# Two more hidden tiles ahead in each feed-forward input, a new load order for its output stage, and adaLN one block later

## The chip, the cores and the metric

One core of a Trainium2 chip runs the whole program. The metric is the device time of one execution in microseconds (us). TensorE (PE, its weight load PEld) multiplies matrices, VectorE (DVE), ScalarE (ACT) and GpSimd (POOL) work on elements, and SyncE (SP) issues all transfers of this program.

## What is computed

A trunk of two layers over 1024 frames of width 1024, everything in float32. Each layer has a mixer sublayer and a feed-forward sublayer, and each sublayer normalizes, shifts and scales by columns that come from the conditioning vector c (adaLN), and adds its gated result to x:

```python
cond = jax.nn.silu(c)
for layer in range(DEPTH):
    mod = cond @ ada_w[layer] + ada_b[layer]
    sh1, sc1, g1, sh2, sc2, g2 = jnp.split(mod, 6, axis=-1)
    h = modulate(rms_norm(x, ln_mix_g[layer]), sh1, sc1)
    ...
    x = x + g1[:, None, :] * mix
    h = modulate(rms_norm(x, ln_ffn_g[layer]), sh2, sc2)
    x = x + g2[:, None, :] * swiglu(h, ffn_w_in[layer], ffn_w_out[layer])

def swiglu(h, w_in, w_out):
    gate, up = jnp.split(h @ w_in, 2, axis=-1)
    return (jax.nn.silu(gate) * up) @ w_out
```

The hidden width is 2816, that is 22 tiles of 128. The mixers (attention and a state-space model in layer 0, retention and stick-breaking attention in layer 1) aren't touched by the change.

## The kernel before

**Layout.** x is kept transposed: eight tiles of 128 channels by 1024 frames. Each float32 operand of a product is split into a high and a low part of the type fp32r, and a product is three matmuls (`mm3`, lines 305 to 309): high by high, high by low, low by high. The split of an operand is a cast on ScalarE for the high part and a subtraction on POOL or VectorE for the low part.

**Weights.** `Stream` (lines 103 to 200) loads weights in the order of `plan` (line 266) into four `raw` buffers that it shares with the adaLN loads, and splits them into six `whl` buffers (lines 169 and 170). Each tick of `Pipe` (line 52) pumps it: it splits what has landed as far as `whl` buffers are free, and asks for loads as long as fewer than two wait.

**Feed-forward input.** For each hidden tile m of 128, `ffn_in` (line 1434) computes gate and up of both halves of the frames as a two by two block product in the manner of Strassen and Winograd: seven products in place of eight. Each is one call of `prod` (line 1406): four pairs of channels, three matmuls each, so 12 matmuls of 128x512. The weight sides are A11, A12, A22 and the sums S1 to S4 that `Comb.raw` (line 210) makes on VectorE (line 218); `Comb.make` splits them (lines 227 and 228) in groups of one or two, one `whl` buffer a group. The frame sides are the split normalized first half (HT, columns 0 to 511), and for the second half the sums T1 (kept in HT, channels 0 to 3), T2, T3, T4 and the second half itself (HT, channels 4 to 7). `norm_t` (line 416) makes these for the four pairs of channels, one after the other, with VectorE for the sums and `put` (line 428) for the splits, whose subtractions alternate between POOL and VectorE. All combine through PSUM banks: three of tag `mm`, four of tag `at`. The results go to memory as `ad` (line 1450).

**The early tiles.** A11 and A12 need only the first half of the frames. While the second half is being normalized, `ffn_first` (line 1410) does these two products for the first EARLY = 3 tiles, first all three of A11, then all three of A12, from weights loaded a second time as whole units (`wfirst`). Their sums stay in SBUF as `p1` and `sg`, three buffers each. `ffn_in` then does five products for these tiles (S2, S3, S1, A22, S4) and seven for the others.

**Feed-forward output.** `ffn_out` (line 1499) takes the hidden tiles in blocks of two, and four in the last block. For each block, half of the frames and output tile n it accumulates 6 matmuls in a bank and adds the bank to x (line 1537). The hidden tiles come back from `ad` into the eight HT buffers (line 1509), the last four into other buffers (line 1518), and x from `xd` into buffers that held T2 to T4 (line 1527). All these are issued on SP.

**adaLN.** `ada` (line 336) makes one of the six columns of a layer: eight loads of 512 KB, each multiplied into an accumulator on VectorE (lines 345 and 347), one a tick, then two ticks on a product with ones on TensorE (line 353). During layer 0's output stage `run` (line 1607) makes five columns of layer 1, one after the other; it is started ahead of the stage.

**What sets the order.** The program text gives the order in which the steps are written, with generators that advance by ticks. The tile framework then plans the order on each engine and queue with a clock of its own, within the data's and buffers' dependencies. Each engine and SP's queue run strictly in the planned order.

Of the kernel before, what the change touches and what calls it, by code (L numbers as in the profile page):

```python
# [17 lines left out]
P = 128  # L18
D = 1024
T = 1024  # L20
# [4 lines left out]
FB = 2  # L25
EARLY = 3
EPS = 1e-6
# [210 lines left out]
class Trunk:  # L238
    def __init__(self, ctx, tc, I, out):
# [17 lines left out]
        for name, shape in (("mixd", [NK, P, T]), ("cad", [P, 16, 2, P]), ("m2d", [P, 16, 2, P]), ("ed", [P, 16, 2, P]),  # L257
                            ("m1d", [P, 32, P]), ("kd", [16, 32, 16, 16]), ("ytd", [4, P, T]), ("vd", [8, P, NT, 64]),
                            ("qkd", [4, 2, 2, P, T]), ("xd", [NK, P, T]), ("ad", [NH, P, 2, T]), ("ud", [8, P, 512])):
            setattr(self, name, self.dr.tile(shape, F32, name=name))  # L260
# [5 lines left out]
    def plan(self):  # L266
# [11 lines left out]
        def ffn(l):  # L278
            w = I["ffn_w_in"][l]
            self.wfirst.append([st.unit(w[m].rearrange("p (k u c) -> p k u c", k=NK, u=2)[:, :, 0]) for m in range(EARLY)])  # L280
            some, full = (("S2", "S3"), ("S1", "A22"), ("S4",)), (("A11", "A12"), ("S2", "S3"), ("S1", "A22"), ("S4",))
            self.win.append([st.pairs(w[m], some if m < EARLY else full, m > 0) for m in range(NH)])
            self.wfo.append([st.unit(I["ffn_w_out"][l, m * P:(m + 1) * P, :]) for m in range(NH)])
# [52 lines left out]
    def ada(self, pool, layer, part):  # L336
# [3 lines left out]
        for k in range(NK + 1):  # L340
# [8 lines left out]
            yield 1  # L349
        yield 2  # L350
        ps = self.at_bank()
# [64 lines left out]
    def norm_t(self, pool, fp, ar, x, sb):  # L416
# [16 lines left out]
        for p in range(4):  # L433
# [9 lines left out]
            v.tensor_sub(t1, h12, b11.hi.bitcast(F32))  # L443
            v.tensor_sub(t1, t1, b11.lo.bitcast(F32))
            v.tensor_sub(t2, h22, t1)
            put(self.T[2][p], t2)
            v.tensor_sub(h12, h22, h12)
            put(self.T[3][p], h12)
            put(self.HT[:, p, sl], t1)
            v.tensor_sub(t4, b21.hi.bitcast(F32), t2)  # L450
# [959 lines left out]
    def ffn_first(self, layer, fp):  # L1410

        nc, pipe = self.nc, self.pipe
        first = slice(0, 512)
        w = [c.k(0) for c in self.wfirst[layer]]
        self.p1, self.sg = {}, {}
        for m in range(EARLY):
            ps = self.mm_bank()
            self.prod(ps, w[m], [self.HT[:, p, first] for p in range(4)])
            self.p1[m] = fp.tile([P, 512], F32, tag="p1", bufs=EARLY, name="p1")
            nc.scalar.copy(self.p1[m], ps)  # L1420
            pipe.tick()
        for m in range(EARLY):
            ps = self.mm_bank()
            self.prod(ps, w[m][:, 512:], [self.HT[:, 4 + p, first] for p in range(4)])
            self.gate(fp, m, self.p1[m], ps)
            self.wfirst[layer][m].free()
            pipe.tick()

    def gate(self, fp, m, p1, p2):
        self.sg[m] = fp.tile([P, 512], F32, tag="sg", bufs=EARLY, name="sg")  # L1430
        self.nc.vector.tensor_add(self.sg[m], p1, p2)
        self.nc.scalar.activation(self.sg[m], self.sg[m], AF.Silu)

    def ffn_in(self, layer, fp, tp):
# [8 lines left out]
        def tmp():  # L1443
            return fp.tile([P, 512], F32, tag="u", bufs=4, name="u")
# [7 lines left out]
        for m in range(NH):  # L1452
            w = self.win[layer][m]
            early = m < EARLY
            if not early:
                a = self.mm_bank()
                self.prod(a, w.get("A11"), b11)
                self.p1[m] = fp.tile([P, 512], F32, tag="p1", bufs=EARLY, name="p1")
                nc.scalar.copy(self.p1[m], a)
                pipe.tick()  # L1460
                a = self.mm_bank()
                self.prod(a, w.get("A12"), b21)
                self.gate(fp, m, self.p1[m], a)
                w.free("A12")
                pipe.tick()
            b = self.mm_bank()
            self.prod(b, w.get("S2"), self.T[2])
            u = tmp()
            v.tensor_add(u, self.p1[m], b)
            pipe.tick()  # L1470
            c = self.at_bank()
            self.prod(c, w.get("S3"), self.T[3])
            c22 = tmp()
            v.tensor_add(c22, u, c)
            w.free("S3")
            pipe.tick()
            d = self.at_bank()
            self.prod(d, w.get("S1"), t1)
            c21, c22 = c22, tmp()
            v.tensor_add(c22, c21, d)  # L1480
# [17 lines left out]

    def ffn_out(self, pool, ar, layer, x, done):

# [19 lines left out]

        for m in range(NK):
            load(m)
        for n in range(NK):
            k = n // 2 + n % 2 * 4
            x[k] = ar.tile([P, T], F32, tag="ar", bufs=12, name="x")
        for n in range(NK):
            nc.sync.dma_start(out=x[n], in_=self.xd[n])
        for bi, ms in enumerate(blocks):
            last = bi + 1 == len(blocks)
            for h in range(2):  # L1530
                sl = slice(h * 512, h * 512 + 512)
# [21 lines left out]
def build(ctx, tc, I, out):  # L1553
# [37 lines left out]
    def half_layer(layer, ar, x, late, before, done, adas=()):  # L1591
# [13 lines left out]
        with tc.tile_pool(name=f"ph2{layer}", bufs=1, reuse_waits="tile") as p2:  # L1605
# [4 lines left out]

            pipe.start(run())
            k.ffn_out(p2, ar, layer, x, lambda n, h: done(p2, n, h))
            if layer == 0:
# [142 lines left out]
```

## Time and profile before

| | us |
|---|---|
| median of 3 runs | 2605.24 |
| lowest, highest | 2605.15, 2607.04 |
| the profiled execution | 2606.74 |
| its span, first to last instruction | 2605.0 |

| engine | busy us | share of the span |
|---|---|---|
| TensorE | 2449.5 | 94% |
| VectorE | 1562.7 | 60% |
| POOL | 1091.8 | 42% |
| ScalarE | 890.8 | 34% |

The profile is of one execution. A row of the timeline gives the start and the length of an instruction and, in brackets, how long the engine stood idle before it and what released it. Matmuls overlap, so their lengths exceed the distance between their starts, and the distance is what counts. The granted clock is a share of 2.4 GHz; the other level, 1.2 GHz, reads 0.50, and a stretch with both lies between.

### The profile page before, as it was taken

The page shows a single profiled execution, that of the slowest core. Times are in us where ns is not written, and L with a number is a line of the kernel's source. Part 1 is how long each engine was busy: PE and PEld are TensorE (multiplying, and loading weights), DVE is VectorE, ACT ScalarE, POOL GpSimd, SP SyncE. Part 2 cuts the span into 40 slices and gives each one's busy share as a digit, 9 for nine tenths or more (in the row PEclk, how much of TensorE's full clock was granted, in tenths as well). Part 3 has the DMA queues.
Part 4 walks back from the last instruction along what each step waited for, and adds up shares of the span by engine and source line. Part 5 has one row for each costly group of instructions (what it writes and reads, how often), then busy time and mean ns, then how long its engine had stood idle before and what let it go on. Part 6 is the DMA issues. An engine that isn't in the chain of part 4 may idle for free. (4 is left out here: it accounts for less than half of the span.)

```text
span 2605.0 us, 33520 instructions
## 1 busy us (share of the span) xinstructions
PE 2449.5 (94%) x12384; PEld 2029.7 (78%) x12384; DVE 1562.7 (60%) x2474; ACT 890.8 (34%) x1679; POOL 1091.8 (42%) x772
## 2 busy tenths in 40 slices
PE   6999898997999998799999999999979999998999
PEld 4898676875888887578788788877758888887887
DVE  6576564368766663576541466666587666654553
ACT  4332467524333332000232344444244333331000
POOL 3465102436776765121123134243148676662220
PEclk9999999998999999899999999999989999999999
DMA  7287764541333336864145332234523333339311
GB/s 284 90 243 222 198 183 155 197 162 57 122 117 110 114 113 259 323 236 152 63 124 173 97 102 83 61 104 135 171 73 114 105 113 113 107 131 364 145 45 65
DMA packets 189812, 379.40 MB, mean 146 GB/s; under 512 B 37264, under 2 KB 91216, under 8 KB 184272
## 3 DMA queue, kind: packets, MB, share of 16 engines
q1 hardware_dynamic: 189648, 377.26, 43.0%
q8 instruction: 98, 1.61, 0.3%
q14 instruction: 66, 0.54, 0.1%
HBM read 278.89 MB, written 100.40 MB: 146 GB/s over the span
## 5 line engine op out<-in xcount | busy, mean ns | idle before, releaser
L170 POOL TENSOR_TENSOR whl<-raw,whl 128x1024 fp32r<-128x1024 f32 x98 | 242.1, 2489 | 602.4 <-ACT whl L169 505.7
L1537 DVE SCALAR_TENSOR_TENSOR x<-at,col,x 128x512 f32<-128x512 f32 x320 | 236.5, 749 | 196.9 <-PE at L309 196.8
L228 POOL TENSOR_TENSOR whl<-sw,whl 128x512 fp32r<-128x512 f32 x176 | 266.7, 1526 | 67.6 <-ACT whl L227 67.6
L307 PE MATMUL at<-a,whl 128*128 128x512 f32 x704 | 279.4, 397 | 16.4 <-DMA a<-ad 13.8
L308 PE MATMUL at<-a,whl 128*128 128x512 f32 x704 | 277.4, 394 | 0.0
L309 PE MATMUL at<-a,whl 128*128 128x512 f32 x704 | 277.0, 393 | 0.0
L308 PE MATMUL mm<-HT,whl 128*128 128x512 f32 x688 | 270.1, 393 | 0.2
L307 PE MATMUL mm<-HT,whl 128*128 128x512 f32 x688 | 268.8, 393 | 1.2 <-ACT p L1420 1.1
L309 PE MATMUL mm<-HT,whl 128*128 128x512 f32 x688 | 269.2, 392 | 0.0
L169 ACT CAST whl<-raw 128x1024 fp32r<-128x1024 f32 x116 | 119.3, 1052 | 437.1 <-PE at L309 200.6
L307 PE MATMUL mm<-whl,HT 128*128 128x512 f32 (+1 forms) x688 | 249.9, 364 | 9.7 <-ACT HT L504 9.2
L308 PE MATMUL mm<-whl,HT 128*128 128x512 f32 (+1 forms) x688 | 246.0, 358 | 0.0
L309 PE MATMUL mm<-whl,HT 128*128 128x512 f32 (+1 forms) x688 | 243.5, 358 | 0.0
L228 POOL TENSOR_TENSOR whl<-raw,whl 128x512 fp32r<-128x512 f32 x120 | 178.2, 1497 | 138.8 <-ACT whl L227 138.8
L218 DVE TENSOR_TENSOR sw<-raw 128x512 f32<-128x512 f32 x88 | 144.1, 1638 | 63.0 <-POOL whl L228 61.4
L307 PEld LDWEIGHTS at<-a,whl 128*128 128x128 f32 x704 | 134.3, 191 | 47.7 <-issue 14.9
L227 ACT CAST whl<-sw 128x512 fp32r<-128x512 f32 x176 | 104.9, 620 | 165.5 <-PE at L309 111.7
L307 PEld LDWEIGHTS mm<-whl,HT 128*128 128x128 f32 x688 | 138.3, 201 | 26.9 <-ACT HT L504 11.9
L309 PEld LDWEIGHTS at<-a,whl 128*128 128x128 f32 x704 | 134.2, 191 | 28.4
L308 PEld LDWEIGHTS at<-a,whl 128*128 128x128 f32 x704 | 134.3, 191 | 27.9 <-issue 0.2
L308 PE MATMUL at<-HT,whl 128*128 128x512 f32 x384 | 151.9, 396 | 0.9 <-DVE HT L430 0.9
L307 PEld LDWEIGHTS mm<-HT,whl 128*128 128x128 f32 x688 | 130.1, 189 | 29.0 <-ACT p L1420 1.6
(343 smaller groups left out, 5380.5 us busy)
## 6 DMA issues: line engine op xcount, KB each, us to landing
raw<-in_ffn_w_in SPq DMA_DIRECT2D x94, 512.0 KB, 3.6
ad<-aT SPq DMA_DIRECT2D x88, 512.0 KB, 3.0
raw<-in_ada_w SPq DMA_DIRECT2D x80, 512.0 KB, 4.6
a<-ad SPq DMA_DIRECT2D x36, 1024.0 KB, 10.7
raw<-in_ffn_w_out SPq DMA_DIRECT2D x44, 512.0 KB, 4.1
xd<-x SPq DMA_DIRECT2D x24, 512.0 KB, 2.7
x<-xd SPq DMA_DIRECT2D x24, 512.0 KB, 8.2
ada<-in_ada SPq DMA_DIRECT2D x16, 512.0 KB, 10.7
```

The lines of the kernel that those rows point to most:

```text
L169: nc.scalar.copy(hi, u.raw[:, :u.n])
L170: self.low.tensor_sub(lo, u.raw[:, :u.n], hi.bitcast(F32))
L218: self.stream.t.nc.vector.tensor_tensor(t, a, b, op)
L227: nc.scalar.copy(hi, z)
L228: nc.gpsimd.tensor_sub(lo, z, hi.bitcast(F32))
L307: mm(out, lhs.hi, rhs.hi, start=start, stop=False)
L308: mm(out, lhs.hi, rhs.lo, start=False, stop=False)
L309: mm(out, lhs.lo, rhs.hi, start=False, stop=stop)
L1537: nc.vector.scalar_tensor_tensor(xh, ps, self.col[layer, 5][:, n:n + 1], xh, M, A)
```

## The change

EARLY is 5 in place of 3. `ffn_first` weaves the products: A11 of tile m, then A12 of tile m - 1. `p1` and `sg` keep three buffers each; the results of all five tiles are stored to a tensor `pd` in memory, and `back` loads them again one tile ahead of their use. S1 is computed first of a tile's later products, T1 is split first in `norm_t`, and the groups become (S1, S2), (S3, A22), (S4). `ffn_out` loads a[0] and a[1], the first halves of x, a[2] and a[3], the second halves of x, then a[4] to a[7]. The chain of five adaLN columns starts with the second block of the output stage, and every adaLN column's product on TensorE comes a tick later.

```diff
-EARLY = 3
+EARLY = 5
...
+("pd", [EARLY, 2, P, 512]),
...
-            some, full = (("S2", "S3"), ("S1", "A22"), ("S4",)), (("A11", "A12"), ("S2", "S3"), ("S1", "A22"), ("S4",))
+            some, full = (("S1", "S2"), ("S3", "A22"), ("S4",)), (("A11", "A12"), ("S1", "S2"), ("S3", "A22"), ("S4",))
...
-        yield 2
+        yield 3
...
             v.tensor_sub(t1, t1, b11.lo.bitcast(F32))
+            put(self.HT[:, p, sl], t1)
             v.tensor_sub(t2, h22, t1)
             put(self.T[2][p], t2)
             v.tensor_sub(h12, h22, h12)
             put(self.T[3][p], h12)
-            put(self.HT[:, p, sl], t1)
...
-        for m in range(EARLY):
-            ps = self.mm_bank()
-            self.prod(ps, w[m], [self.HT[:, p, first] for p in range(4)])
-            self.p1[m] = fp.tile([P, 512], F32, tag="p1", bufs=EARLY, name="p1")
-            nc.scalar.copy(self.p1[m], ps)
-            pipe.tick()
-        for m in range(EARLY):
-            ps = self.mm_bank()
-            self.prod(ps, w[m][:, 512:], [self.HT[:, 4 + p, first] for p in range(4)])
-            self.gate(fp, m, self.p1[m], ps)
-            self.wfirst[layer][m].free()
-            pipe.tick()
+        for m in range(EARLY + 1):
+            if m < EARLY:
+                ps = self.mm_bank()
+                self.prod(ps, w[m], [self.HT[:, p, first] for p in range(4)])
+                self.p1[m] = fp.tile([P, 512], F32, tag="p1", bufs=3, name="p1")
+                nc.scalar.copy(self.p1[m], ps)
+                nc.sync.dma_start(out=self.pd[m, 0], in_=self.p1[m])
+                pipe.tick()
+            if m:
+                ps = self.mm_bank()
+                self.prod(ps, w[m - 1][:, 512:], [self.HT[:, 4 + p, first] for p in range(4)])
+                self.gate(fp, m - 1, self.p1[m - 1], ps)
+                nc.sync.dma_start(out=self.pd[m - 1, 1], in_=self.sg[m - 1])
+                self.wfirst[layer][m - 1].free()
+                pipe.tick()
+        self.back(fp, 0)
+
+    def back(self, fp, m):
+
+        if m < EARLY:
+            self.p1[m], self.sg[m] = (fp.tile([P, 512], F32, tag=t, bufs=3, name=t) for t in ("p1", "sg"))
+            for j, t in enumerate((self.p1[m], self.sg[m])):
+                self.nc.sync.dma_start(out=t, in_=self.pd[m, j])
...
         for m in range(NH):
             w = self.win[layer][m]
             early = m < EARLY
+            self.back(fp, m + 1)
...
+            d = self.at_bank()
+            self.prod(d, w.get("S1"), t1)
+            pipe.tick()
             b = self.mm_bank()
             self.prod(b, w.get("S2"), self.T[2])
             u = tmp()
             v.tensor_add(u, self.p1[m], b)
+            w.free("S2")
             pipe.tick()
             c = self.at_bank()
             self.prod(c, w.get("S3"), self.T[3])
-            c22 = tmp()
-            v.tensor_add(c22, u, c)
-            w.free("S3")
-            pipe.tick()
-            d = self.at_bank()
-            self.prod(d, w.get("S1"), t1)
-            c21, c22 = c22, tmp()
+            c21, c22 = tmp(), tmp()
+            v.tensor_add(c21, u, c)
             v.tensor_add(c22, c21, d)
             v.tensor_add(u, u, d)
             pipe.tick()
...
-        for m in range(NK):
-            load(m)
         for n in range(NK):
             k = n // 2 + n % 2 * 4
             x[k] = ar.tile([P, T], F32, tag="ar", bufs=12, name="x")
-        for n in range(NK):
-            nc.sync.dma_start(out=x[n], in_=self.xd[n])
+        for h in range(2):
+            for m in range(2 * h, 2 * h + 2):
+                load(m)
+            for n in range(NK):
+                nc.sync.dma_start(out=x[n][:, h * 512:h * 512 + 512], in_=self.xd[n, :, h * 512:h * 512 + 512])
+        for m in range(4, NK):
+            load(m)
         for bi, ms in enumerate(blocks):
             last = bi + 1 == len(blocks)
+            if bi == 1:
+                pipe.start(extra)
...
-            pipe.start(run())
-            k.ffn_out(p2, ar, layer, x, lambda n, h: done(p2, n, h))
+            k.ffn_out(p2, ar, layer, x, lambda n, h: done(p2, n, h), run())
```

## Rows read from the trace of the kernel before

**Rows 1.** The page's busy shares: busy us, share of the span, instructions.
```profile
PE 2449.5 (94%) x12384; PEld 2029.7 (78%) x12384; DVE 1562.7 (60%) x2474; ACT 890.8 (34%) x1679; POOL 1091.8 (42%) x772
```

**Rows 2.** What TensorE waited for: us in total, times, longest us.
```profile
PE mm L307 <- ACT T L429: 23.3, 4, 10.0
PE at L353 <- DVE ada L347: 17.9, 1, 17.9
...
PE at L307 <- DMA a<-ad: 13.8, 2, 7.1
```

**Rows 3.** Windows, each: PE, PEld, DVE, ACT, POOL busy us, clock, DMA share, GB/s.
```profile
622.00:632.00 10.00, 10.00 (x34) 8.02 (x33) 7.90 (x13) 5.39 (x9) 3.98 (x3) 0.72 0.00 0
...
658.00:677.00 19.00, 19.00 (x86) 15.73 (x85) 14.66 (x16) 6.74 (x12) 15.69 (x12) 1.00 0.39 139
```

**Rows 4.** Timeline of TensorE, layer 0, from the early products to the T stage.
```profile
592.86 0.39 PE L308 MATMUL mm<-HT,whl 128*128 128x512 f32 x1
593.09 0.40 PE L309 MATMUL mm<-HT,whl 128*128 128x512 f32 x1
...
604.38 1.22 PE L307 MATMUL mm<-T,whl 128*128 128x512 f32 x2 [10.03 <-ACT T L429]
```

**Rows 5.** Timeline of TensorE: output stages of layer 0 and 1, line 353 between.
```profile
1026.84 0.77 PE L307 MATMUL at<-a,whl 128*128 128x512 f32 x1 [6.74 <-DMA a<-ad]
...
1030.59 0.39 PE L307 MATMUL at<-a,whl 128*128 128x512 f32 x1
...
1076.55 3.57 PE L353 MATMUL at<-ones,ada 128*128 128x1 f32 x16 [17.90 <-DVE ada L347]
...
1085.12 0.40 PE L307 MATMUL at<-a,whl 128*128 128x512 f32 x1
...
2358.74 0.77 PE L307 MATMUL at<-a,whl 128*128 128x512 f32 x1 [7.09 <-DMA a<-ad]
...
2365.12 0.40 PE L307 MATMUL at<-a,whl 128*128 128x512 f32 x1
```

**Rows 6.** Timeline of TensorE, the same place in layer 1.
```profile
1936.21 1.22 PE L307 MATMUL mm<-T,whl 128*128 128x512 f32 x2 [9.46 <-ACT T L429]
```

**Rows 7.** Timeline of VectorE, layer 0, the T stage.
```profile
596.35 2.05 DVE L436 SCALAR_TENSOR_TENSOR nf<-x,col,at 128x512 f32<-128x512 f32 x3
...
600.24 1.76 DVE L447 TENSOR_TENSOR nf<-nf 128x512 f32<-128x512 f32 x1
...
607.96 0.68 DVE L447 TENSOR_TENSOR nf<-nf 128x512 f32<-128x512 f32 x1
...
629.22 0.68 DVE L451 TENSOR_TENSOR tn<-tn,HT 128x512 f32<-128x512 f32 x1
```

**Rows 8.** Windows, columns as in rows 3; under them one DMA issue of 1010:1070.
```profile
1010.00:1070.00 60.00, 41.92 (x177) 33.95 (x175) 27.31 (x35) 6.93 (x8) 14.97 (x8) 0.87 1.02 405
1080.00:1220.00 140.00, 137.40 (x621) 112.76 (x622) 104.57 (x131) 12.01 (x12) 27.60 (x12) 0.98 0.63 218
...
raw<-in_ada_w SPq DMA_DIRECT2D x8, 512.0 KB, 9.5
```

**Rows 9.** Timeline of SP's queue, layer 0, at the output stage's start.
```profile
1008.09 3.54 SPq L1527 DMA_DIRECT2D x<-xd  x5
...
1014.83 4.67 SPq L1509 DMA_DIRECT2D a<-ad  x4
```

**Rows 10.** Timeline of POOL, layer 0, early products and T stage.
```profile
572.32 3.69 POOL L170 TENSOR_TENSOR whl<-raw,whl 128x1024 fp32r<-128x1024 f32 x1 [16.57 <-ACT whl L169]
...
595.24 1.71 POOL L228 TENSOR_TENSOR whl<-sw,whl 128x512 fp32r<-128x512 f32 x1
...
612.36 1.28 POOL L430 TENSOR_TENSOR T<-nf,T 128x512 fp32r<-128x512 f32 x1 [6.68 <-DVE tn L450]
```

**Rows 11.** The page's DMA issues: count, KB each, median us to landing.
```profile
raw<-in_ffn_w_in SPq DMA_DIRECT2D x94, 512.0 KB, 3.6
ad<-aT SPq DMA_DIRECT2D x88, 512.0 KB, 3.0
```

More of the change, by code (lines that the diff above doesn't have):

```diff
@@ L258, in __init__ @@
                             ("m1d", [P, 32, P]), ("kd", [16, 32, 16, 16]), ("ytd", [4, P, T]), ("vd", [8, P, NT, 64]),
-                            ("qkd", [4, 2, 2, P, T]), ("xd", [NK, P, T]), ("ad", [NH, P, 2, T]), ("ud", [8, P, 512])):
+                            ("qkd", [4, 2, 2, P, T]), ("xd", [NK, P, T]), ("ad", [NH, P, 2, T]), ("pd", [EARLY, 2, P, 512]), ("ud", [8, P, 512])):
             setattr(self, name, self.dr.tile(shape, F32, name=name))
@@ L1415, in ffn_first @@
         self.p1, self.sg = {}, {}
-        for m in range(EARLY):
-            ps = self.mm_bank()
-            self.prod(ps, w[m], [self.HT[:, p, first] for p in range(4)])
-            self.p1[m] = fp.tile([P, 512], F32, tag="p1", bufs=EARLY, name="p1")
-            nc.scalar.copy(self.p1[m], ps)
-            pipe.tick()
-        for m in range(EARLY):
-            ps = self.mm_bank()
-            self.prod(ps, w[m][:, 512:], [self.HT[:, 4 + p, first] for p in range(4)])
-            self.gate(fp, m, self.p1[m], ps)
-            self.wfirst[layer][m].free()
-            pipe.tick()
+        for m in range(EARLY + 1):
[19 more added lines that the diff above has]
+                self.nc.sync.dma_start(out=t, in_=self.pd[m, j])
     def gate(self, fp, m, p1, p2):
-        self.sg[m] = fp.tile([P, 512], F32, tag="sg", bufs=EARLY, name="sg")
+        self.sg[m] = fp.tile([P, 512], F32, tag="sg", bufs=3, name="sg")
         self.nc.vector.tensor_add(self.sg[m], p1, p2)
@@ L1457, in ffn_in @@
                 self.prod(a, w.get("A11"), b11)
-                self.p1[m] = fp.tile([P, 512], F32, tag="p1", bufs=EARLY, name="p1")
+                self.p1[m] = fp.tile([P, 512], F32, tag="p1", bufs=3, name="p1")
                 nc.scalar.copy(self.p1[m], a)
@@ L1497, in ffn_in, with ffn_out @@
             pipe.tick()
-    def ffn_out(self, pool, ar, layer, x, done):
+    def ffn_out(self, pool, ar, layer, x, done, extra):
         nc, pipe = self.nc, self.pipe
```

## The prediction

> **What bounds the kernel now.** First the page's busy shares: TensorE runs 2449.5 of 2605.0 us [rows 1], so the end is set by TensorE and by its holes, and the reader should look for holes. Then the waits of TensorE, longest first [rows 2]: three causes lead. Products that read a T tile wait 23.3 us in four places; the small adaLN product of line 353 waits 17.9 us once; the first product of the output stage waits 13.8 us in two places. They are what the diff touches, and they are priced one by one from the timeline.
>
> The first: at the upper of TensorE's two clock levels, 2.4 GHz (granted 1.00 from 658 to 677 [rows 3]), matmuls start 0.23 us apart [rows 4], so a product of `prod` (12 matmuls) takes 2.8 us; behind a long hole they run for a while at 1.2 GHz, 0.43 us apart [rows 5]. After the six early products TensorE stands 10.03 us in layer 0 [rows 4] and 9.46 us in layer 1 [rows 6]; the rest of the 23.3, 3.8 us, are small holes further on. Behind this stands VectorE: it makes the T tiles from 596.35 to 629.9 with hardly a pause [rows 7]. The second and third lie in one stretch. From 1010 to 1070 the transfers fill the DMA engines (share 1.02, 405 GB/s, in 60 us 24.3 MB) [rows 8]: eight x loads are issued from 1008.09 on, the a tiles only from 1014.83 on [rows 9], and TensorE starts 6.74 us late; layer 1 repeats it with 7.09 us [rows 5]. In that jam lie also the eight adaLN loads of the first of five parts [rows 8], and line 353, placed in TensorE's order by the planner, holds everything behind it for 17.90 us [rows 5].
>
> **The change, part by part. 1: two more tiles early, in both layers.** Nothing is added to TensorE: tiles 3 and 4 do their first two products earlier. The four products are 4 x 12 x 0.23 = 11.0 us of work for a hole of 10.03 and of 9.46 us. If the T tiles come when they came, TensorE is through 11.0 us sooner: the little more than the hole is swallowed by the small holes behind it. S1 ahead of S2 asks for T1, which the norm now splits first; that can only make the first start earlier, and I give it nothing.
>
> What is paid: five early weights hold five of the six `whl` buffers, so of tile 0 only one group fits beside them, and tile 1's groups, which were finished beside the early products (the last subtraction starts at 595.24), get buffers only as the early weights fall free, that is within the T stage. Two more splits of 128x1024 go over POOL, 3.69 us for one here [rows 10]. In the T stage VectorE gets two gate additions and perhaps tile 1's four sums, all of the T operations' shape, and is slowed by five POOL subtractions: such an operation takes 0.68 us, or 1.76 [rows 7]. From below 0 (all of it falls behind the T work), from above 6 x 0.68 = 4.1 and some 2.7 us for half of the five subtractions meeting an operation: 6.8 us. I take 3, nearest to the two additions and two sums without POOL beside them. The other way, the low clock after the hole (0.72 from 622 to 632 [rows 3]) costs 2.8 us there at most. So each layer gains 11 - 3 = 8 us, bounds 4 and 14: **16 us, 8 to 28**.
>
> On why 0.68 becomes 1.76: the Trainium skill, page "SBUF — State Buffer", section "Who interferes with whom", says that a VectorE instruction with two inputs in SBUF and a GpSimd one that reads SBUF shut each other out for a whole instruction. The two lengths of line 447 agree. The rule speaks against this change, as POOL's work moves into the stage that VectorE paces; what it would do at its worst is rival 1.
>
> The spill: ten stores and ten loads of 256 KB a layer. A store of 512 KB lands 3.0 us after issue, a weight load after 3.6 [rows 11]; the loads are asked a tile ahead (five products, 13.8 us), and the DMA engines are mostly idle there (share 0.39 from 658 to 677 [rows 3]). Cost 0, from below 0, from above rival 3. Two more weight loads a layer, the same. In later early tiles TensorE wants a new tile every 13.8 us; POOL has for it five subtractions and two more for the result, 7 x 1.71 = 12.0 [rows 10]: it fits, with little to spare. In 658 to 677 POOL is busy 15.69 of 19 us [rows 3].
>
> **2: the output stage's order.** S1 first means that HT0 to HT3, which a[0] to a[3] go into, are free after the third product of the last tile and not after the fifth: 2 x 2.76 = 5.5 us sooner. Ahead of a[0], a[1] stood 4 MB of x, about 10 us at 405 GB/s; now nothing, and only x halves (2 MB) stand between the first a tiles and the next. a[0] and a[1] land before TensorE ends, the first x halves by the time of the first evacuation; the second halves are wanted 11 us on. Removed: 6.74 us, and the low clock behind it (9 matmuls in 3.75 us for 2.07: 1.7); in layer 1 7.09 us, and 15 matmuls in 6.38 for 3.45: 2.9 [rows 5]. Together 18.4. I keep 2 us for a start that isn't clean: **16 us, 10 to 18.4**; 10 is what the 5.5 us alone would bring in each layer, less clock.
>
> **3: adaLN a block later.** A block of the output stage is 96 matmuls, 22 us; `yield 3` moves line 353 one tick (12 matmuls) further. Line 353 is then wanted some 22 + 12 x 2.8 = 55 us after the stage's start, at about 1075 on the old scale. What must have moved by then is the 24.3 MB of the jam and some 3 MB more, 67 us at 405 GB/s from 1007 on: 1074. So it just fits, and the wait comes out at 0 to 5 us, not 18. The four later parts, with the DMA share at 0.63 [rows 8], have no wait at line 353 at all (one wait in the list [rows 2]). Gone with it: line 353's 16 small matmuls at the low clock (3.57 us, half of that at the high one: 1.8) and 12 matmuls from their end to 1085.12, 5.0 us for 2.8: 2.2 [rows 5]. 17.9 + 1.8 + 2.2 = 21.9, less 3 for a remaining wait: **19 us, 5 to 22**. The chain of five parts now takes 8 + 60 ticks of the stage's 88, so it still ends inside; the other five adaLN calls each end a tick later, at nothing, since none of them is waited for in [rows 2].
>
> **Sum.** 16 + 16 + 19 = 51 us, bounds 23 and 68. The profiled execution took 2606.7 us (its span of 2605.0 and 1.7 around it), so 2555.7; the median of the runs is 1.5 below that execution, so **2554 us**, bounds 2537 and 2582.
>
> **Rivals.** Rival 1, the T stage gives back what the early products bring: tile 1's subtractions and sums land among the T operations and push the last T tile back by the full 11 us. For it: VectorE has no pause there, and the 1.76 us beside POOL. Against: POOL is idle for 6.68 us at a time in that stage [rows 10], and the planner may put the sums behind. Part 1 brings nothing: 35 us, 2570.
>
> Rival 2, the adaLN wait moves on instead of going: the loads still come late, since line 353 is placed by a plan that didn't see the jam. For: the bytes just fit. Against: four later parts at a lower share without a wait. Part 3 brings 2 us: 34, 2571.
>
> Rival 3, on the slower side: the spill blocks SP's queue. A load from `pd` can only go once its store has landed, and everything behind it on SP, the next tile's weight rows above all, waits too. If each of ten early tiles waited for its own store and load, 3.0 + 3.6 = 6.6 us and half as much for the low clock, that is 99 us: 2653. It decides from 5.1 us a tile on, where it eats the 51. Against: the loads are asked 13.8 us ahead. The Trainium skill, page "DMA: Bandwidth & Descriptors", section "Two DMAs through the same engine are not ordered", says that the issuing engine has to wait for the first transfer's semaphore before it issues one that reads its bytes. No row of this trace shows how long SP stands for it.
>
> Rival 4, the change doesn't do what it says: the engines' order comes from the planner, not from the text; TensorE's rows in the T stage mix products of several tiles. If it sets x ahead of a again and the early products behind the T work, only part 3 is left: 19 us, 2587; at worst nothing.
>
> **How the numbers follow.** The forecast has 0.60, rival 1 0.13, rival 2 0.12, rival 3 0.07, rival 4 0.08. The range, 2536 to 2582, takes in the bounds of the sum and rivals 1 and 2. About 0.2%, 5 us, is what a measurement can tell from no change. Faster: 0.60 + 0.13 + 0.12 and 0.05 of rival 4 = 0.90; same: 0.03 of rival 4 and 0.01 of rival 3; slower: 0.06 of rival 3.
>
> **What would show it.** Part 1: ten products back to back before the first that reads T, no hole over 3 us there, the last T operation within 3 us of its old place. Part 2: a[0] and a[1] issued ahead of x, no wait for a at the stage's start. Part 3: line 353 under 5 us. Rival 1 shows as holes in TensorE between the first and the last T tile that grew by about 10 us, rival 3 as waits for `whl` or p1 in the first five tiles. The prediction is wrong if TensorE's waits for T, a and adaLN fall by less than 25 us in sum, or if a new wait of over 10 us stands elsewhere.

## The result: 46.6 us faster, and the profile after

The changed kernel took 2559.09 us (median of 4 runs, 2558.23 to 2563.23) beside 2605.65 us for the kernel before in as many (2605.15 to 2607.04): a ratio of 0.9824, 95% interval 0.9807 to 0.9841. The profiled execution of the changed kernel took 2558.23 us, its span 2556.4.

The page's busy shares of the changed kernel, to be read against [rows 1]:

```profile
PE 2436.9 (95%) x12384; PEld 2017.5 (79%) x12384; DVE 1577.0 (62%) x2474; ACT 889.4 (35%) x1675; POOL 1100.7 (43%) x768
```

TensorE is busy 12.6 us less with the same 12384 matmuls (less time at the low clock: the granted clock is 0.981 over the span, 0.971 before), and VectorE 14.3 us more with the same 2474 instructions. What TensorE waits for after the change (us in total, times, longest us), against [rows 2]:

```profile
PE at L379 <- DVE xacc L523: 16.8, 1, 16.8
PE at L308 <- DVE T L430: 11.4, 4, 4.1
PE at L353 <- DVE ada L347: 10.7, 1, 10.7
...
PE at L307 <- ACT T L429: 3.7, 4, 1.6
PE mm L308 <- POOL T L430: 2.3, 2, 1.6
```

The wait for a is gone from the list. The wait at line 353 fell from 17.9 to 10.7 us, not to 3. In the T stage, all TensorE waits for HT and T parts together fell from 14.2 to 10.4 us in layer 0 and from 14.6 to 9.5 in layer 1 (the sums of this list's lines, cut to the stage), with another releaser in the lead: before it was a T tile's high part from ScalarE, now it is a low part from VectorE.

**Where the gain came from.** Both traces hold 12384 matmuls in the same number per stage, so the start of the n-th one can be compared. What the changed kernel gains in each stretch of n (us, before minus after; the two profiled executions are 48.5 us apart, the medians 46.6):

| stretch | layer 0 | layer 1 | forecast, both |
|---|---|---|---|
| mixers | 2.0 | 4.2 | 0 |
| output projection, norms | 2.3 | 2.9 | 0 |
| early products and T stage (part 1) | 5.0 | 4.4 | 16 |
| rest of the feed-forward input | 0.0 | 0.0 | 0 |
| start of the output stage (part 2) | 8.3 | 9.7 | 16 |
| rest of the output stage (part 3) | 10.0 | 0.0 | 19 |

Part 2 came as forecast, parts 1 and 3 at little more than half. 11.4 us lie in stretches that the forecast left at nothing. The steps of the T stage repeat: the five kernels below that don't differ there (the changed one, adaLN's two other starts, whole x tiles, the loads on ScalarE's queue) have 5.0 us in layer 0 and 4.4 to 4.7 in layer 1.

**The T stage.** Windows of VectorE's T stage, first line 436 to last T operation: the changed kernel (line 451), then the kernel before. Columns as in [rows 3].

```profile
589.10:630.90 41.80, 32.40 (x117) 23.23 (x115) 41.60 (x51) 23.69 (x41) 24.49 (x15) 0.88 0.41 132
```
```profile
596.30:629.90 33.60, 21.33 (x56) 14.36 (x57) 33.49 (x44) 17.52 (x28) 13.34 (x10) 0.64 0.10 31
```

VectorE is full in both, but the stage is 8.2 us longer, with seven more VectorE instructions (four sums of tile 1, three gate additions) and 11 us more of POOL. The timeline shows the two meeting. POOL, then VectorE, changed kernel:

```profile
596.54 3.45 POOL L228 TENSOR_TENSOR whl<-sw,whl 128x512 fp32r<-128x512 f32 x2
599.95 1.73 POOL L430 TENSOR_TENSOR T<-nf,T 128x512 fp32r<-128x512 f32 x1
603.55 1.62 POOL L228 TENSOR_TENSOR whl<-sw,whl 128x512 fp32r<-128x512 f32 x1 [1.87 <-ACT whl L227]
605.14 1.70 POOL L228 TENSOR_TENSOR whl<-raw,whl 128x512 fp32r<-128x512 f32 x1
```
```profile
598.76 1.78 DVE L430 TENSOR_TENSOR T<-tn,T 128x512 fp32r<-128x512 f32 x1
600.46 1.77 DVE L451 TENSOR_TENSOR tn<-tn,HT 128x512 f32<-128x512 f32 x1
602.16 0.68 DVE L218 TENSOR_TENSOR sw<-raw 128x512 f32<-128x512 f32 x1
...
603.96 1.76 DVE L430 TENSOR_TENSOR HT<-nf,HT 128x512 fp32r<-128x512 f32 x1
605.64 1.74 DVE L218 TENSOR_TENSOR sw<-sw,raw 128x512 f32<-128x512 f32 x1
607.31 1.74 DVE L430 TENSOR_TENSOR T<-tn,T 128x512 fp32r<-128x512 f32 x1
```

While POOL subtracts, these VectorE operations, all with both inputs in SBUF, take 1.74 to 1.78 us; in POOL's pause at 602 one takes 0.68. The last one, at 607.31, ends at 609.05, and that is what TensorE stands for longest:

```profile
609.11 0.79 PE L308 MATMUL at<-T,whl 128*128 128x512 f32 x1 [4.11 <-DVE T L430]
```

**The output stage's start.** SP's queue, then TensorE, changed kernel, against [rows 9] and [rows 5]:

```profile
999.09 2.89 SPq L1520 DMA_DIRECT2D a<-ad  x4
1002.08 0.82 SPq L1539 DMA_DIRECT2D x<-xd  x1
```
```profile
1010.65 0.39 PE L309 MATMUL at<-HT,whl 128*128 128x512 f32 x1
1010.88 0.39 PE L307 MATMUL at<-a,whl 128*128 128x512 f32 x1
```

The first four a transfers now leave 11.8 us before they are needed, ahead of x, and TensorE goes over without a gap. The kernel's text puts two of them ahead of x; the planner put all four there.

**Line 353.** The window of the jam (columns as in [rows 3], clock, DMA share and GB/s last), then the chain to line 353 by engine: SP, ScalarE, POOL, VectorE, TensorE, changed kernel.

```profile
1011.00:1070.00 59.00, 54.73 (x241) 44.68 (x239) 35.26 (x46) 6.21 (x7) 16.07 (x8) 0.98 1.02 401
```
```profile
1041.72 1.61 SPq L343 DMA_DIRECT2D raw<-in_ada_w  x2
...
1057.89 13.24 SPq L343 DMA_DIRECT2D raw<-in_ada_w  x6
```
```profile
1054.32 2.00 ACT L169 CAST whl<-raw 128x1024 fp32r<-128x1024 f32 x2 [19.80 <-PE at L309]
```
```profile
1055.46 4.77 POOL L170 TENSOR_TENSOR whl<-raw,whl 128x1024 fp32r<-128x1024 f32 x2 [17.05 <-ACT whl L169]
```
```profile
1061.07 0.74 DVE L345 TENSOR_SCALAR ada<-raw,scond 128x1024 f32<-128x1024 f32 x1
...
1068.17 6.57 DVE L347 SCALAR_TENSOR_TENSOR ada<-raw,scond,ada 128x1024 f32<-128x1024 f32 x5 [1.58 <-DMA raw<-in_ada_w]
```
```profile
1076.46 3.57 PE L353 MATMUL at<-ones,ada 128*128 128x1 f32 x16 [10.66 <-DVE ada L347]
```

TensorE is ready for line 353 at 1065.80, 55 us after the stage's start, as the prediction worked out. Two of the eight loads go at 1041.72, the other six only from 1057.89 on. Four raw buffers serve everything. Two hold the next block's weights, which ScalarE and POOL can split only when `whl` buffers fall free at the block's end: POOL is through the first at about 1057.8, and the third adaLN load goes. The other two hold adaLN loads that had landed by 1056.2, but VectorE's order has their first use at 1061.07. The jam has its part all the same: the third load, issued at 1057.89, landed at 1068.08, 10.2 us later, and VectorE stood 1.58 us for it.

Of the 10.0 us in the rest of the output stage, 7.1 lie around this first column (wait and slow matmuls behind it: 24.2 us before, 17.2 now, beside an unbroken run of matmuls 0.227 us apart) and 3.0 around the four later ones, which the forecast left at nothing.

### The profile page after: what moved, and what is told of

Its sections match the earlier page's. It is cut to its first block, busy times and chain, and to the rows that moved or that the text cites. A ratio compares the mean times of both kernels' runs of the same rounds, so it can differ in the third digit from the quotient of the medians.

```text
span 2556.4 us, 33613 instructions
## 1 busy us (share of the span) xinstructions
PE 2436.9 (95%) x12384; PEld 2017.5 (79%) x12384; DVE 1577.0 (62%) x2474; ACT 889.4 (35%) x1675; POOL 1100.7 (43%) x768
## 5 line engine op out<-in xcount | busy, mean ns | idle before, releaser
L170 POOL TENSOR_TENSOR whl<-raw,whl 128x1024 fp32r<-128x1024 f32 x102 | 253.2, 2502 | 570.1 <-ACT whl L169 540.6
L228 POOL TENSOR_TENSOR whl<-raw,whl 128x512 fp32r<-128x512 f32 x112 | 164.5, 1481 | 128.2 <-ACT whl L227 128.2
## 6 DMA issues: line engine op xcount, KB each, us to landing
ada<-in_ada SPq DMA_DIRECT2D x16, 512.0 KB, 10.4
```

The costliest lines, as they stand in the source:

```text
L170: self.low.tensor_sub(lo, u.raw[:, :u.n], hi.bitcast(F32))
L228: nc.gpsimd.tensor_sub(lo, z, hi.bitcast(F32))
```

## The experiments

Each is an edit of the changed kernel. Steps are gains against the kernel before in the same stretches of n as in the table; the changed kernel's own steps are those of the table. Each kernel has one trace.

**adaLN started yet a block later.**

```diff
-            if bi == 1:
+            if bi == 2:
```

> The changed kernel with the adaLN chain started at the third block of the output stage instead of the second. Theory (the 10.66 us still waited at line 353 come from the transfers queued at the stage's start, 24 MB in 60 us, which the first adaLN loads sit behind): another 22 us later the queue has run empty, the wait at line 353 falls under 2 us, and with the low clock behind it the kernel takes 11 to 13 us less than the changed one, 2547. Rival (the planner sets line 353 ahead of its data wherever the chain starts): a wait of 8 us or more stands again, 2556 to 2560.

2556.11 us (2552.61 to 2560.22), ratio 0.9807 [0.9787, 0.9827]. The wait at line 353 is still 7.05 us, between what the theory (under 2) and the rival (8 or more) had said. Window, SP, VectorE, TensorE of this kernel:

```profile
1060.00:1070.00 10.00, 10.00 (x46) 8.29 (x45) 5.74 (x8) 0.00 (x0) 0.00 (x0) 1.00 0.41 162
```
```profile
1054.64 2.69 SPq L343 DMA_DIRECT2D raw<-in_ada_w  x2
1072.79 1.01 SPq L1520 DMA_DIRECT2D a<-ad  x2
1073.90 11.89 SPq L343 DMA_DIRECT2D raw<-in_ada_w  x6
```
```profile
1072.79 0.75 DVE L345 TENSOR_SCALAR ada<-raw,scond 128x1024 f32<-128x1024 f32 x1
```
```profile
1091.37 3.57 PE L353 MATMUL at<-ones,ada 128*128 128x1 f32 x16 [7.05 <-DVE ada L347]
```

The DMA engines are at a share of 0.41 for ten us, with loads waiting to be issued: the jam is over, and the chain is still late. So the jam's bytes, on which the prediction built, are not all that sets this wait. The loads come two at first and six after the block's end, the same pattern one block later. Here SP itself stood from 1057.3 to 1072.79, for the a load ahead of the third adaLN load; whether the queue is the cause is what the run on ScalarE's queue is for.

**adaLN started ahead of the stage, as before.**

```diff
-            if bi == 1:
+            if bi == 0:
```

> The changed kernel with the adaLN chain started ahead of the output stage again, one block earlier, all else kept. Theory (each block of 22 us later takes some 8 to 10 us off the wait, since the same bytes have to move by then): the wait at line 353 is 16 to 20 us, 2566 to 2570. Rival (the new load order, not the start, shortened the wait): 9 to 12 us, 2558 to 2561.

2576.61 us (2576.21 to 2577.7), ratio 0.9886 [0.9866, 0.9906], slower than both expectations. TensorE (the row counts 13 of the 16 small matmuls, as the window asked for ends there):

```profile
1067.29 2.93 PE L353 MATMUL at<-ones,ada 128*128 128x1 f32 x13 [24.33 <-DVE ada L347]
```

The wait is longer than the 17.90 of the kernel before, and than the 16 to 20 expected: the start of the stage is clean (step 8.6), TensorE comes to line 353 earlier, and the loads don't. The rest of the output stage steps by -7.5 us where the changed kernel gains 10.0, so the later start is worth 17.5 us on top of part 2. The two parts don't add up one by one; part 2 alone would have handed most of its gain in layer 0 to line 353.

**Whole x tiles, behind all eight a tiles.**

```diff
-        for h in range(2):
-            for m in range(2 * h, 2 * h + 2):
-                load(m)
-            for n in range(NK):
-                nc.sync.dma_start(out=x[n][:, h * 512:h * 512 + 512], in_=self.xd[n, :, h * 512:h * 512 + 512])
-        for m in range(4, NK):
+        for m in range(NK):
             load(m)
+        for n in range(NK):
+            nc.sync.dma_start(out=x[n], in_=self.xd[n])
```

> The changed kernel with the output stage's loads as before: eight a tiles, then eight whole x tiles; S1 stays first. Theory (a[0] to a[3] come in time because S1 first frees HT0 to HT3 earlier, and the halves of x do nothing that the four banks don't cover): no wait for a at the stage's start, at most 2 us for x, 2558 to 2562. Rival (the halves are what let TensorE start at once): a wait of 4 us or more at each of the two starts, with the low clock behind it 2570 or more.

2561.51 us (2556.24 to 2565.07), ratio 0.9825 [0.9804, 0.9847]; the start steps by 7.6 and 9.1 us where the changed kernel has 8.3 and 9.7. SP's queue shows the same order at its head:

```profile
996.17 3.54 SPq L1520 DMA_DIRECT2D a<-ad  x4
999.79 0.69 SPq L1538 DMA_DIRECT2D x<-xd  x1
```

No wait for a comes back. With S1 first the halves are worth some 0.6 us a layer.

**S1 third, as before; all else of the change kept.**

```diff
-            some, full = (("S1", "S2"), ("S3", "A22"), ("S4",)), (("A11", "A12"), ("S1", "S2"), ("S3", "A22"), ("S4",))
+            some, full = (("S2", "S3"), ("S1", "A22"), ("S4",)), (("A11", "A12"), ("S2", "S3"), ("S1", "A22"), ("S4",))
...
-            put(self.HT[:, p, sl], t1)
...
             put(self.T[3][p], h12)
+            put(self.HT[:, p, sl], t1)
...
```

> The changed kernel with S1 third again (products S2, S3, S1, groups (S2, S3), (S1, A22), and T1 split after T3); halves of x kept. Theory (HT0 to HT3 come free 5.5 us later): a[0] lands 4 to 6 us later against TensorE, a wait of 2 to 6 us stands at both starts of the output stage, with the clock 2564 to 2574; the T stage changes by under 2 us a layer. Rival (S1's place matters in the T stage alone): no wait at the output stage, under 2562, and the first product that reads T starts 2 us later or more.

2568.78 us (2563.31 to 2574.73), ratio 0.9855 [0.9831, 0.988]. TensorE at the stage's start:

```profile
1016.97 0.76 PE L307 MATMUL at<-a,whl 128*128 128x512 f32 x1 [3.68 <-DMA a<-ad]
```

Layer 1 has a wait of 4.52 us there. The starts step by 3.1 and 4.1, so S1 first is worth 5.2 and 5.6 us a layer, the 5.5 us of two products that the prediction counted. What is left, 3.1 and 4.1, fits the halves of x, though no run shows it by itself: in layer 0 of this kernel SP issues ten halves (2.6 MB) ahead of the first a, in the kernel before eight whole tiles (4.2 MB), and the difference is 3.9 us at the 405 GB/s of [rows 8], an estimate. Where S1 is first, no x stands ahead of a, and the halves bring little. In the T stage the steps are 6.3 and 6.3, that is 1.3 and 1.9 us better than with S1 first: T1 as the first operand wanted costs time there.

**Three early tiles, and three without the spill.** The first is one number; the second also leaves out the stores to `pd` and the loads from it, with `p1` and `sg` kept in their three buffers.

```diff
-EARLY = 5
+EARLY = 3
```
```diff
-                nc.sync.dma_start(out=self.pd[m, 0], in_=self.p1[m])
...
-                nc.sync.dma_start(out=self.pd[m - 1, 1], in_=self.sg[m - 1])
...
-        self.back(fp, 0)
...
-            self.back(fp, m + 1)
```

> The changed kernel with EARLY = 3, all else kept, the spill too. Theory (the two more early tiles bring 11.0 us of filling a layer, and the T stage, longer by 5 us, takes 5 back): 6 us a layer, 12 us slower than the changed kernel, 2571; VectorE's T stage falls back from 41.7 to about 34 us. Rival 1 (the early tiles bring the whole 11 us a layer, the loss sits elsewhere): 2580 or more. Rival 2 (they bring nothing): 2557 to 2561.

> The same with EARLY = 3 and without the spill: the stores to and loads from pd are gone, p1 and sg stay in SBUF as in the kernel before. It prices the spill by itself against early3. Theory (the transfers lie beside other work): within 1.5 us of early3. Rival (SP's queue stands for the round trip): 3 us or more faster than early3.

With the spill 2571.4 us (2568.19 to 2574.93), ratio 0.9862 [0.984, 0.9883]; without it 2581.32 us (2571.69 to 2587.01), ratio 0.9896 [0.9866, 0.9925]. TensorE behind the early products, first with, then without the spill:

```profile
593.37 0.80 PE L307 MATMUL at<-HT,whl 128*128 128x512 f32 x1 [5.49 <-ACT HT L429]
596.72 1.22 PE L307 MATMUL mm<-T,whl 128*128 128x512 f32 x2 [2.55 <-ACT T L429]
```
```profile
598.83 0.80 PE L307 MATMUL at<-HT,whl 128*128 128x512 f32 x1 [5.49 <-ACT HT L429]
602.17 1.22 PE L307 MATMUL mm<-T,whl 128*128 128x512 f32 x2 [2.55 <-ACT T L429]
```

The holes are the same and so are the steps of the T stage, 1.0 and 0.5 us in both. So with three early tiles the spill costs nothing in this stage, and what else the change does to it (the weave, S1 first, T1's earlier split) brings 1.0 and 0.5 us: the rest of part 1's gain is the two added tiles. In all, the kernel without the spill was expected within 1.5 us of the other and is 10 us slower by the medians, with intervals that overlap. In the traces the difference lies in stretches that have no spill (4.0 us in layer 0's mixers, 6.3 in the rest of its output stage, 4.1 in layer 1's output projection); its cause is open.

**Four and six early tiles.**

```diff
-EARLY = 5
+EARLY = 4
```
```diff
-EARLY = 5
+EARLY = 6
```

> The changed kernel with EARLY = 4. Theory (each early tile fills 5.5 us of a hole of 10 and puts its share of work into the T stage): between early3 and the changed kernel, 2562 to 2568, and VectorE's T stage 36 to 40 us long. Rival (the stretch of the T stage comes from the six weight buffers being full, which four early tiles don't reach): the T stage stays at 34 to 36 us, and it takes 2560 or less.

> The changed kernel with EARLY = 6: all six weight buffers go to early tiles. Theory (the hole is filled already with five; a sixth tile only moves more of tile 0's and tile 1's preparation into the T stage): TensorE's early products end 5.5 us later, the T stage ends 3 to 6 us later, 2556 to 2564. Rival (TensorE's waits inside the T stage, some 10 us a layer, are filled by more early work): 2548 to 2553.

2570.97 us (2569.41 to 2580.35), ratio 0.9872 [0.9843, 0.99], and 2561.89 us (2553.87 to 2565.82), ratio 0.9821 [0.9795, 0.9847]. Four tiles are slower than the 2562 to 2568 expected, six lie inside their range. With the changed kernel between them they make a series:

| early tiles | T stage on VectorE, us | step, layer 0 | step, layer 1 |
|---|---|---|---|
| 3 | 34.1 | 1.0 | 0.5 |
| 4 | 38.0 | 2.7 | 2.2 |
| 5 | 41.7 | 5.0 | 4.4 |
| 6 | 43.4 | 6.2 | 5.2 |

(Six: 7.5 and 6.6 in the stage, less 1.3 and 1.4 in the rest of the feed-forward input.) A tile puts 5.5 us of products into the hole and brings 0.8 to 2.3. The T stage grows with each by 1.7 to 3.9 us: the hole fills, and its end moves away.

**POOL taken out of tile 1's splits.** The low parts of tile 1's groups are copied by ScalarE instead of subtracted on POOL. This kernel leaves out the subtraction, so these low parts hold the full value.

```diff
+        off = any(self is w[1] for w in self.stream.t.win)
...
-            nc.gpsimd.tensor_sub(lo, z, hi.bitcast(F32))
+            if off:
+                nc.scalar.copy(lo, z)
+            else:
+                nc.gpsimd.tensor_sub(lo, z, hi.bitcast(F32))
```

> The changed kernel, but the low parts of tile 1's weights are copied by ScalarE and not subtracted by POOL, in both layers (their values are then wrong: the low part holds the full value). VectorE's work is the same. Theory 1 (POOL's five subtractions of tile 1, now in the T stage, hold up VectorE's operations there, 1.75 us for 0.68): VectorE's T stage shrinks from 41.7 us by 3 to 6, and the feed-forward input of each layer gains 2 to 5 us. Theory 2 (the stage is longer for VectorE's own added work, four sums and the gate additions): it stays at 40 us or more and the input gains under 1 us.

2551.82 us (2549.51 to 2556.68), ratio 0.9788 [0.9775, 0.9802]. The window of the T stage, then VectorE in it, this kernel (its lines stand 4 further down, so line 434 is 430 and 455 is 451):

```profile
590.00:627.10 37.10, 31.03 (x117) 22.77 (x115) 36.92 (x51) 25.80 (x45) 17.35 (x10) 0.91 0.47 149
```
```profile
600.27 0.68 DVE L455 TENSOR_TENSOR tn<-tn,HT 128x512 f32<-128x512 f32 x1
600.87 0.68 DVE L434 TENSOR_TENSOR T<-tn,T 128x512 fp32r<-128x512 f32 x1
```

As many VectorE instructions as before take 36.92 us in place of 41.60, with 7.1 us less of POOL beside them; what took 1.77 us takes 0.68. The steps are 9.2 and 9.3 us, so POOL's five subtractions cost 4.2 and 4.9 us a layer. The Trainium skill, page "SBUF — State Buffer", section "Who interferes with whom", says that GpSimd's ports to SBUF are VectorE's second pair, under an exclusive lock; the two lengths, 1.77 and 0.68 us, agree with it.

**adaLN's loads on ScalarE's queue.** The loads of the five columns are issued there, so that they stand behind nothing on SP.

```diff
-                nc.sync.dma_start(out=nxt, in_=self.I["ada_w"][layer, k * P:(k + 1) * P, part * D:(part + 1) * D])
+                (nc.scalar if layer == 1 and part != 5 else nc.sync).dma_start(out=nxt, in_=self.I["ada_w"][layer, k * P:(k + 1) * P, part * D:(part + 1) * D])
```

> The changed kernel with the loads of the five adaLN parts in the output stage issued on ScalarE's queue and not on SP's. Theory (the third and later loads stand in SP's queue behind a-loads that wait for TensorE to end a block and free an HT buffer): they go out earlier, the wait of 10.66 us at line 353 falls under 4 us, and the output stage of layer 0 gains 7 to 12 us. Rival (they wait for one of the four raw buffers, which VectorE and POOL free, whichever queue they stand in): the wait stays at 8 us or more.

2559.68 us (2556.84 to 2563.6), ratio 0.9817 [0.9803, 0.9831]. ScalarE's own work and its queue, then TensorE:

```profile
1043.54 1.64 ACTq L343 DMA_DIRECT2D raw<-in_ada_w  x2
1055.55 2.00 ACT L169 CAST whl<-raw 128x1024 fp32r<-128x1024 f32 x2 [19.76 <-PE at L309]
1059.17 18.10 ACTq L343 DMA_DIRECT2D raw<-in_ada_w  x8
```
```profile
1076.96 3.57 PE L353 MATMUL at<-ones,ada 128*128 128x1 f32 x16 [9.88 <-DVE ada L347]
```

9.88 us in place of 10.66: what SP's queue holds ahead of these loads explains 0.8 us at most. The third load still goes as the first raw buffer comes free behind the split at the block's end.

**Two findings put together.** S1 third in all tiles but the last, which alone feeds the output stage; and the first column's product eight ticks behind its last load's use, in place of three.

```diff
-        yield 3
+        yield 8 if (layer, part) == (1, 1) else 3
...
+            last = m == NH - 1
+            if last:
+                d = self.at_bank()
+                self.prod(d, w.get("S1"), t1)
```

> A version put together: the changed kernel with S1 third and T1 split after T3 as in the kernel before, but S1 first in the last tile of each layer; and the first of the five adaLN parts asks for its product on TensorE five ticks later (yield 8). Theory: the starts of the output stage keep their gain, 8 to 10 us each; the feed-forward inputs gain 1.3 and 1.9 us as they did with S1 third; five ticks are 13.8 us and the wait at line 353 is 10.66, so it goes to 0 to 1 us and takes the low clock behind it along, 11 to 13 us. Together 2542 to 2548. Rival (the planner moves the loads along with the product): a wait of 6 us or more at line 353, 2552 or more.

2559.57 us (2555.63 to 2564.53), ratio 0.9814 [0.9799, 0.983]. TensorE, VectorE and SP at line 353:

```profile
1089.06 3.57 PE L353 MATMUL at<-ones,ada 128*128 128x1 f32 x16 [8.72 <-DVE ada L347]
```
```profile
1076.96 1.28 DVE L347 SCALAR_TENSOR_TENSOR ada<-raw,scond,ada 128x1024 f32<-128x1024 f32 x1
...
1087.72 1.28 DVE L347 SCALAR_TENSOR_TENSOR ada<-raw,scond,ada 128x1024 f32<-128x1024 f32 x1 [0.68 <-DMA raw<-in_ada_w]
```
```profile
1058.83 6.17 SPq L343 DMA_DIRECT2D raw<-in_ada_w  x4
1078.27 2.19 SPq L343 DMA_DIRECT2D raw<-in_ada_w  x2
```

The T stage gains 1.7 and 1.9 us over the changed kernel, as the S1 run had it, and the starts are kept (8.5 and 9.5). But line 353 moved 12.6 us back and still waits 8.72: its sums on VectorE moved back too, the last from 1075.12 to 1087.72. The output stage steps by 6.7 in place of 10.0, and nothing is left in the total: the rival's case. Here the trace shows what held the loads. The third to sixth had landed at 1068.88 to 1072.68 and filled all four raw buffers; VectorE's order read the third only at 1076.96, and only then could the last two be issued, at 1078.27 and 1080.12.

**adaLN's product a tick sooner, as before.**

```diff
-        yield 3
+        yield 2
```

> The changed kernel with yield 2 again in the adaLN columns, the start at the second block kept. Theory (a tick is 12 matmuls, 2.8 us, and the loads don't depend on it): the wait at line 353 is 13 to 14 us, the output stage of layer 0 takes 3 us more. Rival (the tick changes nothing, the planner places line 353 by its data): 10 to 11.5 us.

2574.51 us (2572.01 to 2578.63), ratio 0.9875 [0.9861, 0.9889]: by the ratios 13 us slower than the changed kernel. TensorE's wait at line 353 (us in total, times, longest us):

```profile
PE at L353 <- DVE ada L347: 13.5, 1, 13.5
```

Line 353 waits 2.8 us longer, one tick, and the rest of the output stage gains 5.9 us less: 3.8 around the first column, 2.1 around the four later ones. The T stages step by 3.7 and 3.2 (1.3 and 1.2 less), below all five kernels that share this stage otherwise (5.0, and 4.4 to 4.7). The output projections step by -0.3 and -0.4 (2.6 and 3.3 less), but there nothing is shown: among the kernels with the third tick this step goes from -0.5 to 6.6 in layer 0 and from -2.2 to 3.4 in layer 1.

## Why the prediction was right, and where its terms were off

**The whole.** 2554 was forecast and 2559.09 measured, inside the range. The three mechanisms are there. The sum is better than its terms: 51 us came out as 18.0 + 9.4 + 10.0 = 37.4 in the places forecast, and 11.4 us in the mixers and output projections made up for much of the rest. That the total lands 5 us from the forecast is thus in part luck. In these two stretches the steps of the thirteen kernels with the change or a part of it go from -2.2 to 6.6 us with one trace each, so that gain can't be called the change's. TensorE's waits for T, a and adaLN fell by some 30 us in sum (8.8, 13.8 and 7.2), not far above the 25 below which the prediction called itself wrong.

**Part 2, 16 forecast, 18.0 measured: right.** The a transfers leave first, TensorE goes over without a gap, and the low clock behind the hole is gone (granted 0.98 from 1011 to 1070, 0.87 before [rows 8]). The 18.4 us worked out from [rows 5] were closer than the 2 us taken off for an unclean start. The 5.5 us of two products were found as 5.2 and 5.6 in the run with S1 third. The halves of x, which the prediction built on as well, are worth 0.6 us: all four a transfers leave ahead of them.

**Part 1, 16 forecast, 9.4 measured: mechanism right, the cost too small.** The ten early products run, and no hole of 10 us is left. The mis-sized term is what is paid for the 11.0 us of work: 3 us a layer taken, 6.0 and 6.6 measured (11.0 less 5.0 and 4.4), near the 6.8 us that was worked out as its upper bound. That bound had the right parts, six operations (there are seven) and five subtractions, and it was set aside in favour of the row without POOL beside it. The run without these subtractions shows that they alone cost 4.2 and 4.9 us. A second term was put at nothing: S1 first "can only make the first start earlier", but with S1 third the T stage steps 1.3 and 1.9 us better. The two costs need not add up. VectorE had no pause in [rows 7], so whatever lengthens one of its operations there lengthens the stage. Rival 1 was right in kind, tile 1's sums and subtractions do push the T tiles back, but not by the full 11 us: TensorE's holes behind the first product that reads T grew from 4.2 to 10.2 us in layer 0 and from 5.1 to 9.3 in layer 1.

The test that the prediction set was met by its letter: no hole over 1 us among the early products and up to the first product that reads T (at 602.94 in layer 0), and the last T operation at 630.16, 0.94 us behind its old place in the span. It looked in the wrong place: the hole of 4.11 us opens 6 us later, at 609.11, and since VectorE began its T stage 7.2 us earlier (589.13 for 596.35), an end at the old place hides the 8.2 us that the stage grew by.

**Part 3, 19 forecast, 10.0 measured: the failing step is the remaining wait.** Only 7.1 of the 10.0 lie where the forecast had its 19, at the first column. It said that 67 us of transfers fit before line 353 and leave 3 us. Line 353 was wanted when it said, and 10.66 us were left. The step took the DMA engines as the only thing in the way of the loads. They are full (share 1.02), and a load issued late takes 10.2 us to land there, but with a share of 0.41 in the run a block later 7.05 us remain, on another queue 9.88, and with the product five ticks later 8.72. What stays the same in all four is that two loads go early and the others only when POOL and VectorE have worked off four shared raw buffers at the block's end. That the later columns had no wait at line 353 in [rows 2] was read as proof that a free DMA is enough; the first column differs from them in more than that. Rival 2, that the wait moves on, is thus half true, for another cause than the one it named. In the changed kernel it is open whether the buffers alone or the planned place of VectorE's first use (1061.07, 4.9 us behind the landing of the pair) decides: a kernel with more raw buffers wasn't tried. In the run of two findings put together it is VectorE's place, with four landed loads waiting for it.

**The tick at nothing.** That "the other five adaLN calls each end a tick later, at nothing" is the other weak step. Without the third tick the kernel is 13 us slower in the total, by the ratios. In the traces 5.9 of it lie in the rest of layer 0's output stage, where the tick was counted, and 1.3 and 1.2 in the T stages, where it wasn't and where [rows 2] has no wait for adaLN to show it. By what path the tick reaches the T stages is open, and so is the remainder.

**Rival 3, the spill, is out.** With three early tiles the T stage steps the same with it and without it; with five there is no run without it, but its sign, waits for `whl` or p1 in the first five tiles, comes to 0.2 us a layer. In 560 to 700 SP's queue waited for a store to `pd` like this (us in total, times, longest us):

```profile
SPq L1438 <- DVE u L1484: 20.3, 2, 15.6
...
SPq L1438 <- DMA pd<-sg: 4.7, 2, 3.2
```

So SP does stand still for the store, 4.7 us in two places, and 20.3 us for a buffer of p1. TensorE doesn't feel it: no wait of TensorE there names a load. The Trainium skill, page "DMA: Bandwidth & Descriptors", section "Two DMAs through the same engine are not ordered", has it that the issuing engine waits for the first transfer's semaphore; the row agrees. Rival 4 is out too: the ten early products stand ahead of the T work, and SP's order differs from the text in that four a transfers and not two go ahead of x.

## What to carry to other kernels

Work that fills a hole of TensorE brings its supporting work along; cost each subtraction, addition and load at the engine that paces the stage, at its length beside the other engines and not at its best one. Before a late result is blamed on transfers, look at when its loads were issued and which buffer they waited for. When one wait is taken away ahead of another, reckon the second one anew, and compare the starts of the n-th matmul rather than sums of waits, so that a gain from elsewhere isn't booked to the change.

## What the runs showed of the hardware

- A VectorE addition of 128x512 with both inputs in SBUF takes 0.68 us alone and, in the rows shown, 1.74 to 1.78 us beside a POOL subtraction. Five such subtractions, 8.5 us in all, made VectorE's stage 4.7 us longer (41.60 against 36.92 us busy). An addition with an input in a PSUM bank isn't lengthened: the 44 gate additions of line 1442 take 0.67 to 0.69 us each, 42 of them with POOL busy all along.
- The 256 KB transfers of half an x tile and the 512 KB ones of a whole one brought almost the same start (8.3 against 7.6 us gained), and the jam that holds the halves ran at 401 GB/s, the one that held the whole tiles at 405 [rows 8].
- An engine's queue in planned order can hold a landed load unread: the first adaLN load landed at 1054.9 and was read at 1061.07, in the run a block later it landed at 1065.2 and was read at 1072.79, and in the run of two findings put together the third landed at 1068.9 and was read at 1076.96.
